# A fourth summed weight piece in every other gate-and-up unit, and summed pieces in half of u and in z

## The chip, the cores and the metric

The kernel runs on one core of one Trainium2 chip. The time is that of the device in microseconds (us). Engines are named as in the profile: PE is TensorE (matmuls; PEld its weight loads), DVE is VectorE, ACT is ScalarE, POOL is GpSimd, SP is SyncE, which here only issues DMAs.

## The reference

One layer of a hybrid decoder trunk, on 256 tokens of width 2048, all in float32:

```
h = x + 1/2 * SwiGLU_1(RMSNorm(x))                      # d_ff 5632: [2048 -> 2 x 5632], [5632 -> 2048]
P = RMSNorm(h) @ W_in                                   # columns: u 2048 | v 2048 | z 2048 | x 2048 | B 1024 | C 1024 | dt 32
a = gelu(u) * (W_s RMSNorm(gelu(v)) + b)                # causal mixing inside chunks of 128 tokens
m = RMSNorm(SSD(conv(x, B, C), dt) * SiLU(z))           # Mamba-2 chunked scan, 2 chunks of 128 tokens, 32 heads of 64
h = h + concat([a, m]) @ W_out
h = h + CrossAttn(RMSNorm(h), RMSNorm(mem))             # 4 heads of 512 into 256 memory tokens
h = h + 1/2 * SwiGLU_2(RMSNorm(h))
out = RMSNorm(h)
```

Weight gains of the norms and the conv's weights are left out here. The time goes into the big matrix products.

## The kernel before

**Products in three matmuls.** A float32 number is held as a rounded high part (type fp32r) and a remainder, the low part. A product of two such matrices takes three matmuls: high x high, high x low, low x high. Weights come from memory as float32 into a buffer `raw`; ScalarE writes the high part (`high`, L159 to L162) and VectorE the low part (`low`, L171 to L174, through `split_op`, which keeps these operations in the order in which they are written). Tokens are the stationary operand and weights the moving one, 512 columns a matmul. TensorE gets its instructions in program order (`pe`, L69).

**Units and pieces.** `proj_sum` (L245) works through one *unit*: two column blocks of 512 weights (j = 0, 1; gate and up, in an FFN) times two blocks of 128 tokens (t = 0, 1), over a contraction of 2048 in eight *pieces* of 256 (k = 0, 1, of 128 each). A piece is of one of two kinds.

- *C, plain*: the eight products (t, j, k), each of three matmuls: 24. One high and one low operation on 128x2048 weights.
- *S, summed*: Strassen and Winograd's scheme for 2 x 2 blocks, seven products, m1 to m7, for eight: 21 matmuls. For it VectorE makes four sums of the four weight blocks (tile `sum`, three operations), and highs and lows are made of three raw blocks and of the four sums (`split_sums`, L189). The token operand has the same sums, made beforehand (`Pieces.sums`, L415); its first four forms are the plain blocks, so that `tokens` (L239) can also read an S operand as a plain one.

Products m1, m6, m5, m7 each gather in a PSUM bank over all S pieces of the unit and are combined after the last of them (`mid`, four VectorE additions in `parts_of`); m2, m3, m4 gather in the banks of the plain results. In an S piece the products come in the order m1, m2, m3, m6, m5, m7, m4, in the last S of a unit m1, m6, m5, m7, m2, m3, m4 (L268 to L270). m1, m2 and m3 read raw weight blocks, the other four read sums. The unit ends with a C, in which each of the four results is evacuated (`evac`).

**Buffers.** Each pool has a fixed number of buffers, and a tile that is asked for waits until all that read the buffer's last content are done:

```
    wraw = ctx.enter_context(tc.tile_pool(name="wraw", bufs=3))
    whigh = ctx.enter_context(tc.tile_pool(name="whigh", bufs=3))
    wlow = ctx.enter_context(tc.tile_pool(name="wlow", bufs=2))
    wsum = ctx.enter_context(tc.tile_pool(name="wsum", bufs=1))
    wshigh = ctx.enter_context(tc.tile_pool(name="wshigh", bufs=1))
    wslow = ctx.enter_context(tc.tile_pool(name="wslow", bufs=1))
    big = ctx.enter_context(tc.tile_pool(name="big", bufs=12))
```

wsum, wshigh and wslow hold the sums of an S piece, their high and their low parts. `big` holds token operands and activations in twelve slots of 8 KB a partition; an S operand takes a slot, a C operand half of one.

**Order of work.** The kinds of a unit's pieces stand in a string, one letter for each piece of the contraction, and an order list says in which order the pieces are taken. GU_KINDS with GU_ORDER gives C C S C S C S C for all units of the FFNs but the first. An FFN has eleven units (c = 0 to 10); after five and after the other six, a down projection (`add_sum`, two halves) takes up their ten and twelve pieces. Small jobs (transposes that make the next operands, the steps of the scan) are put off with `later(fn, by)` by so many pieces, and `step` carries them out between pieces, but not between the first and the last S of a unit, when all PSUM banks are taken.

**The middle.** After FFN 1 come B, C and x (`proj_feat`), then v, u and z (`proj_tok`, all plain, eight pieces a half of 1024 columns, two halves each). The scan of the SSD runs beside v and u: `scan_start` (t, j) fetches a tile `dec` by a DMA of 1 MB and makes decays and scores, `scan_apply` does the matmuls yp and, at the end, yo. Then the output projection, the queries, the memory's keys and values, the attention and its output, and FFN 2.

Of the kernel before, what the change touches and what calls it, by code (L numbers as in the profile page):

```python
# [46 lines left out]
def hybrid_layer(ctx: ExitStack, tc: tile.TileContext, x, mem, w_gu1, w_dn1, w_in, w_s, w_out,  # L47
# [24 lines left out]
    def matmul(out, lhsT, rhs, start=False, stop=False):  # L72
        return pe(nc.tensor.matmul(out, lhsT=lhsT, rhs=rhs, start=start, stop=stop))  # L73
# [130 lines left out]
    def proj_tok(w, r0, xts, cs, evac, kts=D // P):  # L204

        n = kts // KP
        ps = {}
        for i in range(n):
            hi, lo = split(load(w, r0 + i * KP * P, cs, PLAIN))
            order = [(t, k) for k in range(KP) for t in range(NT)]  # L210
            if i in (0, n - 1):
                order.sort()
            for t, k in order:
                if t not in ps:
                    ps[t] = [side("acc") for _ in range(2)]
                kt = i * KP + k
                xt = xts[kt // KG][:, kt % KG, :]
                xh, xl = xt[:, t * P:(t + 1) * P], xt[:, S + t * P:S + (t + 1) * P]
# [106 lines left out]
        junk = half_k(F32, "junk")  # L325
        return nc.scalar.activation(junk, src, AF.Square, accum_out=ss)

    def rstd_of(ss, name):
        n = ss.shape[1]
        r = small.tile([P, n], F32, name=f"rstd_{name}", bufs=1)  # L330
        ms = small.tile([P, n], F32, name="ms")
        nc.vector.tensor_reduce(out=ms, in_=ss, axis=AX.X, op=ALU.add)
# [105 lines left out]
    class Normed:  # L438


        def __init__(self, name, c0, kinds=None, bys=None):
            self.bys = bys
            self.name, self.c0 = name, c0
            self.xts = [] if kinds is None else Pieces(kinds, f"xp_{name}")
            self.ss = small.tile([P, NT, 4], F32, name=f"ss_{name}", bufs=1)

        def chunk(self, n, by=1):
            srcs = [h[n][:, t, :] for t in range(NT)]
# [10 lines left out]
        def stats(self, n):  # L459
            for t in range(NT):  # L460
                sum_sq(self.ss[:, t, n:n + 1], h[n][:, t, :])
            if n == 3:
                self.rstd = rstd_of(self.ss, self.name)

    def axpy(y, a, x):
        return nc.vector.scalar_tensor_tensor(out=y, in0=x, scalar=a, in1=y, op0=ALU.mult, op1=ALU.add)
# [38 lines left out]
        nc.vector.tensor_tensor(out=out, in0=a, in1=b, op=op)  # L505
# [129 lines left out]
    def raw_dts():  # L635
# [5 lines left out]
        nc.vector.tensor_tensor(out=wd[:, :, HEADS:], in0=raw_dt, in1=wd[:, :, :HEADS].bitcast(F32), op=ALU.subtract)  # L641
        pdt = side("dt")
        for k in range(D // P):
            matmul(pdt[:2 * HEADS, :], wd[:, k, :], nx.xts[k // KG][:, k % KG, :],
                   start=(k == 0), stop=(k == D // P - 1))
        dtf = half_k(F32, "dtf")
        nc.scalar.copy(out=dtf[:2 * HEADS, :], in_=pdt[:2 * HEADS, :])
# [101 lines left out]
    dend = small.tile([P, HEADS], F32, name="dend", bufs=1)  # L749
    scan = {}  # L750

    def scan_start(t, j):
        hs = slice(j * 16, j * 16 + 16)
        if j == 0:
            scan["xdt"] = scan[f"xdt{t}"] = xdt = slot([P, HEADS, HD], F32, "xdt")
            nc.vector.tensor_tensor(out=xdt, in0=y[t], in1=per_head(dt[:, t, :], HD), op=ALU.mult)
            nc.vector.tensor_tensor(out=y[t], in0=y[t], in1=per_head(rowb[:, 2, :], HD), op=ALU.mult)
        dec = slot([P, 16, P], F32, "dec")
        nc.gpsimd.dma_start(
            out=dec.rearrange("p h l -> p (h l)"),  # L760
            in_=cum_rows[t:t + 1, j * 16 * P:(j + 1) * 16 * P].broadcast_to([P, 16 * P]))
# [101 lines left out]
    for c in (0, 2):  # L863
        gss = [[], []]

        def evac(t, ps):
            for j in range(2):
                g = half_k(F32, "gate")
                nc.scalar.activation(g, ps[j], AF.Gelu_apprx_tanh, scale=rstd[:, t:t + 1])
                nc.vector.scalar_tensor_tensor(out=g, in0=v[t][:, c + j, :],  # L870
                                               scalar=col[:, C_GB + c + j:C_GB + c + j + 1],
                                               in1=g, op0=ALU.add, op1=ALU.mult)
                gss[j].append(g)

        proj_tok(w_in, 0, nx.xts, (U0 + c * NC, U0 + (c + 1) * NC), evac)
        for j in range(2):
            ats.later(gss[j], by=1 + j)

    ss_m = small.tile([P, NT, 4], F32, name="ss_m", bufs=1)
    for c in (0, 2):  # L880
        def evac(t, ps):
            for j in range(2):
                g = half_k(F32, "gate")
                nc.scalar.activation(g, ps[j], AF.Silu, scale=rstd[:, t:t + 1])
                ys = y[t][:, (c + j) * 8:(c + j + 1) * 8, :].rearrange("p h d -> p (h d)")
                nc.vector.tensor_tensor(out=ys, in0=ys, in1=g, op=ALU.mult)
                sum_sq(ss_m[:, t, c + j:c + j + 1], ys)
# [44 lines left out]
    def heads(w, xps, kinds, order, c, take):  # L932
        parts = {}

        def mid(banks):
            parts.update(enumerate(parts_of(banks)))

        def evac(t, j, ps):
            x = parts[2 * t + j]
            total(x, ps, x, ALU.subtract if (t, j) == (1, 0) else ALU.add)  # L940
            take(j, t, x)

        proj_sum(w, 0, xps, kinds, (c, c + XD), mid, evac, order)

    MEM_KINDS = "CCCCCCSS"
    XA_ORDER, MEM_ORDER = [0, 1, 2, 5, 3, 7, 4, 6], [0, 1, 2, 6, 3, 7, 4, 5]
    qts, kts, mem_ts = [], [], Pieces(MEM_KINDS, "memt")

    def by_head(to, name):
# [7 lines left out]
        return take  # L957

    for hd in (0, 2):
        heads(w_q, na.xts, XA_KINDS, XA_ORDER, hd * XD, by_head(qts, "qt"))  # L960
# [36 lines left out]
        split_to(pts[hd // 2][:, hd % 2], tps)  # L997

    for hd in (0, 2):
        heads(w_kv, mem_ts, MEM_KINDS, MEM_ORDER, hd * XD, by_head(kts, "kt"))  # L1000
        for j in range(2):
            later(lambda hd=hd + j: attend(hd, kts[hd]), by=2 + j / 2)

# [19 lines left out]
    for hd in (0, 2):  # L1023
# [7 lines left out]
        heads(w_kv, mem_ts, MEM_KINDS, MEM_ORDER, D + hd * XD, take)  # L1031
# [91 lines left out]
```

## Time and profile before

| | |
|---|---|
| median of 2 runs | 2475.26 us (2474.72 to 2475.8) |
| the profiled execution | 2476.08 us, of it the span 2474.4 us |
| PE busy | 2457.2 us, 99% of the span, 11945 matmuls |
| DVE busy | 2027.1 us, 82% |
| ACT busy | 1303.0 us, 53% |
| weights and all else from memory | 472.57 MB read, 192 GB/s |

How to read the profile: times are from the start of the span. A group of instructions is given as line, engine, operation, output <- inputs, shape and count | busy us, mean ns of one | idle time of the engine ahead of them and what ended it. A time line gives start, duration, engine, line, operation and count, with the idle time ahead of it in brackets. The chain that ended last is followed back from the last instruction to what released each step. In a table of windows the row holds the window, its length, then PE, PEld, DVE, ACT and POOL busy (with counts), the granted clock, the DMA share and GB/s. L73 is the line of all matmuls, L161 of `high`, L169 of `split_op`.

### The profile page before, as it was taken

The numbers are of one execution on the slowest core, as the hardware profiler recorded it, in microseconds if no ns is written. First come the engines' busy times: TensorE is split into PE (matmuls) and PEld (weight loads), VectorE is DVE, ScalarE is ACT, GpSimd is POOL, SyncE is SP. The second block draws the span as 40 slices with busy tenths as digits, with TensorE's granted clock in tenths as the row PEclk, the third lists the DMA queues.
The fourth block names the chain that finished last, engine by engine and source line by source line (L and its number), as shares of the span: only waits on it lengthen the run. The fifth ranks groups of instructions, "written<-read, shape, count | busy, mean of one in ns | idle before, by whom it ended". The sixth has DMA issues, their size and how long they took to land.

```text
span 2474.4 us, 30190 instructions
## 1 busy us (share of the span) xinstructions
PE 2457.2 (99%) x11945; PEld 2069.2 (84%) x11945; DVE 2027.1 (82%) x1904; ACT 1303.0 (53%) x1180; POOL 21.0 (1%) x46
## 2 busy tenths in 40 slices
PE   9999999999999999999999999999999999999998
PEld 7888888888899998888888888888888888888886
DVE  7999889999877677655698888778789988899987
ACT  6555445555545454445555655455555544555554
POOL 0000000000000000000000000000000000000000
PEclk9999999999999999999999999999999999999999
DMA  7565665665654555545566555555565656656664
GB/s 241 190 211 191 206 201 192 204 201 190 201 184 162 192 177 202 204 153 187 187 199 227 191 183 170 169 172 185 179 197 193 213 192 202 204 188 204 204 206 151
DMA packets 199870, 476.67 MB, mean 193 GB/s; under 512 B 15296, under 2 KB 17504, under 8 KB 198960
## 3 DMA queue, kind: packets, MB, share of 16 engines
q1 hardware_dynamic: 196912, 464.31, 57.4%
q0 software_dynamic: 1840, 9.26, 1.1%
q8 instruction: 93, 1.52, 0.3%
q10 hardware_dynamic: 976, 1.18, 0.1%
q14 instruction: 49, 0.40, 0.0%
HBM read 472.57 MB, written 2.13 MB: 192 GB/s over the span
## 4 chain that ended last, share of the span: by engine, by line
PE 96%; DVE 2%; ACT 1%; issue 1%; DMA 0%; POOL 0%; DVEq 0%; ACTq 0%; POOLq 0%
PE acc L73 91%; PE tpose L76 2%; DVE lo L169 1%; PE yp L73 1%; ACT hi L161 1%; PE logits L73 0%; PE o L73 0%; DVE cacc L627 0%; PE mixed L73 0%; DMA col<-in_cols 0%; DVE sum L169 0%; PE dt L73 0%; PE scores L73 0%; PE yo L73 0%; PE st L73 0%
## 5 line engine op out<-in xcount | busy, mean ns | idle before, releaser
L161 ACT CAST hi<-raw 128x2048 fp32r<-128x2048 f32 (+1 forms) x438 | 788.2, 1800 | 819.3 <-PE acc L73 724.2
L169 DVE TENSOR_TENSOR lo<-raw,hi 128x2048 fp32r<-128x2048 f32 (+2 forms) x446 | 944.7, 2119 | 238.8 <-PE acc L73 183.8
L73 PE MATMUL acc<-hi,xp_ffn 128*128 128x512 f32 x1824 | 582.3, 392 | 1.5 <-ACT hi L183 1.5
L73 PEld LDWEIGHTS acc<-hi,xp_ffn 128*128 128x128 f32 x1824 | 343.6, 188 | 72.9 <-ACT hi L183 2.2
L73 PE MATMUL acc<-lo,xp_ffn 128*128 128x512 f32 x912 | 356.1, 390 | 0.2 <-DVE lo L169 0.2
L169 DVE TENSOR_TENSOR lo<-sum,hi 128x2048 fp32r<-128x2048 f32 x117 | 268.2, 2292 | 59.4 <-ACT hi L161 59.4
L161 ACT CAST hi<-sum 128x2048 fp32r<-128x2048 f32 x117 | 224.1, 1915 | 119.8 <-DVE sum L169 100.5
L73 PE MATMUL acc<-hi,hid 128*128 128x512 f32 x896 | 282.6, 390 | 0.0
L73 PE MATMUL acc<-hi,xt_mix 128*128 128x512 f32 x768 | 241.7, 393 | 0.0
L73 PEld LDWEIGHTS acc<-lo,xp_ffn 128*128 128x128 f32 x912 | 171.9, 188 | 35.5 <-DVE lo L169 0.7
L505 DVE TENSOR_TENSOR part<-acc,part 128x512 f32<-128x512 f32 x272 | 180.4, 686 | 24.5 <-ACT part L472 9.3
L73 PEld LDWEIGHTS acc<-hi,hid 128*128 128x128 f32 x896 | 168.3, 188 | 34.7
L73 PE MATMUL acc<-xt_mix,hi 128*128 128x256 f32 x1024 | 185.9, 284 | 0.0
L73 PE MATMUL acc<-lo,hid 128*128 128x512 f32 x448 | 174.6, 390 | 0.0
L73 PEld LDWEIGHTS acc<-hi,xt_mix 128*128 128x128 f32 x768 | 144.2, 188 | 30.3 <-issue 0.7
L169 DVE TENSOR_TENSOR sum<-sum,raw 128x512 f32<-128x512 f32 x234 | 161.6, 690 | 6.6
L73 PEld LDWEIGHTS acc<-xt_mix,hi 128*128 128x128 f32 x1024 | 159.6, 192 | 0.3
L73 PE MATMUL acc<-lo,xt_mix 128*128 128x512 f32 x384 | 149.6, 389 | 0.0
L73 PE MATMUL acc<-hi,xp_ffn1s 128*128 128x512 f32 x466 | 148.5, 389 | 0.0
L73 PE MATMUL acc<-hi,xp_ffn2s 128*128 128x512 f32 x466 | 148.5, 389 | 0.0
L73 PE MATMUL acc<-xt_mix,lo 128*128 128x256 f32 x512 | 145.2, 284 | 0.7 <-DVE lo L169 0.7
L169 DVE TENSOR_TENSOR sum<-raw 128x1024 f32<-128x1024 f32 x117 | 142.5, 1218 | 0.0
(280 smaller groups left out, 3205.0 us busy)
## 6 DMA issues: line engine op xcount, KB each, us to landing
raw<-in_w_gu SPq DMA_DIRECT2D x286, 512.0 KB, 4.0
raw<-in_w_in SPq DMA_DIRECT2D x80, 1024.0 KB, 5.2
raw<-in_w_dn SPq DMA_DIRECT2D x60, 1024.0 KB, 5.2
raw<-in_w_gu SPq DMA_DIRECT2D x132, 256.0 KB, 4.1
raw<-in_w_kv SPq DMA_DIRECT2D x24, 1024.0 KB, 5.2
raw<-in_w_out SPq DMA_DIRECT2D x21, 1024.0 KB, 5.2
raw<-in_w_dn SPq DMA_DIRECT2D x28, 512.0 KB, 3.9
raw<-in_w_dn SPq DMA_DIRECT2D x56, 256.0 KB, 4.3
```

The costliest lines, as they stand in the source:

```text
L73: return pe(nc.tensor.matmul(out, lhsT=lhsT, rhs=rhs, start=start, stop=stop))
L76: return pe(nc.tensor.transpose(out=out, in_=in_, identity=identity))
L161: nc.scalar.copy(out=t[:, :n], in_=x[:, :n])
L169: last_split[:] = [nc.vector.tensor_tensor(**kw).ins]
L505: nc.vector.tensor_tensor(out=out, in0=a, in1=b, op=op)
```

## The change

- Units c = 2, 4, 6, 8, 10 of both FFNs: four S pieces for three, in the order C C S S C S S C. Units c = 1, 3, 5, 7, 9 stay at C C S C S C S C; unit 0 stays as it is but reads operand 6, which is now of kind S, as a plain one.
- Down projections of five blocks: two S pieces for three. The FFN's operand (four S, four C) and these ten pieces (two S, eight C) take six slots each.
- The second half of u and both halves of z: `proj_sum` with two S pieces (C C C S C S C C) in place of `proj_tok`, through `column_pair`, which is the `heads` of the attention moved ahead. The operand of the middle becomes a list of Pieces with two S, five slots in place of four; its sums of squares are taken three steps after FFN 1 has ended.
- The scan's starts and applications go from steps 3, 7, 13, 17 and 7, 10, 17, 21 to 5, 8, 15, 18 and 8, 11, 18, 21. Its first two VectorE operations become `scan_inputs`, a step ahead, and `dec` goes from the pool `big` to `wshigh`.
- Queries, keys and values: other orders of the same pieces.

```diff
-    GU_KINDS, GU_ORDER = "CSCSCSCC", [0, 2, 1, 4, 3, 6, 5, 7]
+    GU_KINDS, GU_ORDER = "CSCSCSSC", [0, 2, 1, 4, 3, 6, 5, 7]
+    GU_THREE, MORE_ORDER = "CSCSCSCC", [0, 2, 1, 3, 4, 5, 6, 7]
...
-    DN_KINDS = {5: ("CCSCSCSCCC", None), 6: ("CCCCSCCSCCSS", [0, 1, 4, 2, 10, 3, 7, 5, 11, 6, 8, 9])}
+    DN_KINDS = {5: ("CCSCCSCCCC", None), 6: ("CCCCSCCSCCSS", [0, 1, 4, 2, 10, 3, 7, 5, 11, 6, 8, 9])}
...
                 if c == 0:
                     proj_sum(w_gu, 0, nrm.xts, FIRST_KINDS, (c * NC, DFF + c * NC), mid, evac, FIRST, fine)
+                elif c % 2:
+                    proj_sum(w_gu, 0, nrm.xts, GU_THREE, (c * NC, DFF + c * NC), mid, evac, GU_ORDER)
                 else:
-                    proj_sum(w_gu, 0, nrm.xts, GU_KINDS, (c * NC, DFF + c * NC), mid, evac, GU_ORDER)
+                    proj_sum(w_gu, 0, nrm.xts, GU_KINDS, (c * NC, DFF + c * NC), mid, evac, MORE_ORDER)
...
-    nx = Normed("mix", C_MIX)
+    MIX_KINDS = "CCCSCSCC"
+    nx = Normed("mix", C_MIX, MIX_KINDS, {4: 1, 5: 1, 6: 2, 7: 2})
...
+    def scan_inputs(t):
+        scan["xdt"] = scan[f"xdt{t}"] = xdt = slot([P, HEADS, HD], F32, "xdt")
+        nc.vector.tensor_tensor(out=xdt, in0=y[t], in1=per_head(dt[:, t, :], HD), op=ALU.mult)
+        nc.vector.tensor_tensor(out=y[t], in0=y[t], in1=per_head(rowb[:, 2, :], HD), op=ALU.mult)
...
-        dec = slot([P, 16, P], F32, "dec")
+        dec = wshigh.tile([P, 16, P], F32, name="hi")
...
-    for i, (by, to) in enumerate(((3, 7), (7, 10), (13, 17), (17, 21))):
+    for i, (by, to) in enumerate(((5, 8), (8, 11), (15, 18), (18, 21))):
+        if i % 2 == 0:
+            later(lambda i=i: scan_inputs(i // 2), by=by - 1)
...
-        proj_tok(w_in, 0, nx.xts, (U0 + c * NC, U0 + (c + 1) * NC), evac)
+        if c == 0:
+            proj_tok(w_in, 0, nx.xts, (U0 + c * NC, U0 + (c + 1) * NC), evac)
+        else:
+            column_pair(w_in, nx.xts, MIX_KINDS, None, U0 + c * NC, lambda j, t, x: gate(j, t, x, x))
...
-        proj_tok(w_in, 0, nx.xts, (Z0 + c * NC, Z0 + (c + 1) * NC), evac)
+        column_pair(w_in, nx.xts, MIX_KINDS, None, Z0 + c * NC, take)
...
-    XA_ORDER, MEM_ORDER = [0, 1, 2, 5, 3, 7, 4, 6], [0, 1, 2, 6, 3, 7, 4, 5]
+    XA_ORDER, MEM_ORDER = [0, 1, 2, 3, 5, 4, 7, 6], [0, 1, 2, 3, 6, 4, 7, 5]
```

With the query kinds CCCCCSCS and the memory kinds CCCCCCSS the last line turns C C C S C S C C into C C C C S C S C.

More of the change, by code (lines that the diff above doesn't have):

```diff
@@ L326, in sum_sq, with rstd_of @@
         return nc.scalar.activation(junk, src, AF.Square, accum_out=ss)
-    def rstd_of(ss, name):
+    def rstd_of(ss, name, r=None):
         n = ss.shape[1]
-        r = small.tile([P, n], F32, name=f"rstd_{name}", bufs=1)
+        r = small.tile([P, n], F32, name=f"rstd_{name}", bufs=1) if r is None else r
         ms = small.tile([P, n], F32, name="ms")
@@ L445, in __init__ @@
             self.ss = small.tile([P, NT, 4], F32, name=f"ss_{name}", bufs=1)
+            self.rstd = small.tile([P, NT], F32, name=f"rstd_{name}", bufs=1)
         def chunk(self, n, by=1):
@@ L462, in stats @@
             if n == 3:
-                self.rstd = rstd_of(self.ss, self.name)
+                rstd_of(self.ss, self.name, self.rstd)
     def axpy(y, a, x):
@@ L505, in total, with column_pair, mid, evac @@
         nc.vector.tensor_tensor(out=out, in0=a, in1=b, op=op)
-    GU_KINDS, GU_ORDER = "CSCSCSCC", [0, 2, 1, 4, 3, 6, 5, 7]
+    def column_pair(w, xps, kinds, order, c, take):
+        parts = {}
+        def mid(banks):
+            parts.update(enumerate(parts_of(banks)))
+        def evac(t, j, ps):
+            x = parts[2 * t + j]
+            total(x, ps, x, ALU.subtract if (t, j) == (1, 0) else ALU.add)
+            take(j, t, x)
+        proj_sum(w, 0, xps, kinds, (c, c + NC), mid, evac, order)
+    GU_KINDS, GU_ORDER = "CSCSCSSC", [0, 2, 1, 4, 3, 6, 5, 7]
+    GU_THREE, MORE_ORDER = "CSCSCSCC", [0, 2, 1, 3, 4, 5, 6, 7]
     FIRST_KINDS, FIRST = "CCCCCSCC", [0, 2, 4, 6, 1, 3, 5, 7]
-    DN_KINDS = {5: ("CCSCSCSCCC", None), 6: ("CCCCSCCSCCSS", [0, 1, 4, 2, 10, 3, 7, 5, 11, 6, 8, 9])}
+    DN_KINDS = {5: ("CCSCCSCCCC", None), 6: ("CCCCSCCSCCSS", [0, 1, 4, 2, 10, 3, 7, 5, 11, 6, 8, 9])}
     def ffn(nrm, w_gu, w_dn, done=None, each=None, fine=0):
@@ L643, in raw_dts @@
         for k in range(D // P):
-            matmul(pdt[:2 * HEADS, :], wd[:, k, :], nx.xts[k // KG][:, k % KG, :],
+            x, i = nx.xts[k // KP], k % KP
+            x = x[:, :, 2 * i:2 * i + 2].rearrange("p h f s -> p h (f s)") if len(x.shape) == 4 else \
+                x[:, i].rearrange("p (h s) -> p h s", h=2)
+            matmul(pdt[:2 * HEADS, :].rearrange("p (h s) -> p h s", h=2), wd[:, k, :], x,
                    start=(k == 0), stop=(k == D // P - 1))
@@ L864, in hybrid_layer, with gate @@
         gss = [[], []]
+        def gate(j, t, g, x):
+            nc.scalar.activation(g, x, AF.Gelu_apprx_tanh, scale=rstd[:, t:t + 1])
+            nc.vector.scalar_tensor_tensor(out=g, in0=v[t][:, c + j, :],
+                                           scalar=col[:, C_GB + c + j:C_GB + c + j + 1],
+                                           in1=g, op0=ALU.add, op1=ALU.mult)
+            gss[j].append(g)
         def evac(t, ps):
             for j in range(2):
[L868 to L873, printed above, removed]
-        proj_tok(w_in, 0, nx.xts, (U0 + c * NC, U0 + (c + 1) * NC), evac)
+                gate(j, t, half_k(F32, "gate"), ps[j])
+        if c == 0:
+            proj_tok(w_in, 0, nx.xts, (U0 + c * NC, U0 + (c + 1) * NC), evac)
+        else:
+            column_pair(w_in, nx.xts, MIX_KINDS, None, U0 + c * NC, lambda j, t, x: gate(j, t, x, x))
         for j in range(2):
@@ L880, in hybrid_layer, with take @@
     for c in (0, 2):
[L881 to L887, printed above, removed]
-        proj_tok(w_in, 0, nx.xts, (Z0 + c * NC, Z0 + (c + 1) * NC), evac)
+        def take(j, t, g):
+            nc.scalar.activation(g, g, AF.Silu, scale=rstd[:, t:t + 1])
+            ys = y[t][:, (c + j) * 8:(c + j + 1) * 8, :].rearrange("p h d -> p (h d)")
+            nc.vector.tensor_tensor(out=ys, in0=ys, in1=g, op=ALU.mult)
+            sum_sq(ss_m[:, t, c + j:c + j + 1], ys)
+        column_pair(w_in, nx.xts, MIX_KINDS, None, Z0 + c * NC, take)
     rstd_m = rstd_of(ss_m, "m")
@@ L929, in prep_mem @@
         return ms
[L932 to L943, printed above, removed]
     MEM_KINDS = "CCCCCCSS"
-    XA_ORDER, MEM_ORDER = [0, 1, 2, 5, 3, 7, 4, 6], [0, 1, 2, 6, 3, 7, 4, 5]
+    XA_ORDER, MEM_ORDER = [0, 1, 2, 3, 5, 4, 7, 6], [0, 1, 2, 3, 6, 4, 7, 5]
     qts, kts, mem_ts = [], [], Pieces(MEM_KINDS, "memt")
@@ L959, in hybrid_layer @@
     for hd in (0, 2):
-        heads(w_q, na.xts, XA_KINDS, XA_ORDER, hd * XD, by_head(qts, "qt"))
+        column_pair(w_q, na.xts, XA_KINDS, XA_ORDER, hd * XD, by_head(qts, "qt"))
         if hd == 0:
@@ L999, in hybrid_layer @@
     for hd in (0, 2):
[L1000 removed]
+        column_pair(w_kv, mem_ts, MEM_KINDS, MEM_ORDER, hd * XD, by_head(kts, "kt"))
         for j in range(2):
@@ L1029, in take @@
                                     op=ALU.subtract)
-        heads(w_kv, mem_ts, MEM_KINDS, MEM_ORDER, D + hd * XD, take)
+        column_pair(w_kv, mem_ts, MEM_KINDS, MEM_ORDER, D + hd * XD, take)
         for j in range(2):
```

7 lines of the change are left out of this document (1 added, 6 removed).

## The prediction

> **What bounds the kernel now.** I read the page first: busy times, then the chain that ended last.
>
> ```profile
> PE 2457.2 (99%) x11945; PEld 2069.2 (84%) x11945; DVE 2027.1 (82%) x1904; ACT 1303.0 (53%) x1180; POOL 21.0 (1%) x46
> PE 96%; DVE 2%; ACT 1%; issue 1%; DMA 0%; POOL 0%; DVEq 0%; ACTq 0%; POOLq 0%
> ```
>
> TensorE is the chain (96%) and leaves 2474.4 - 2457.2 = 17.2 us of the span unused. So a matmul that goes saves its time, and a wait that reaches TensorE costs its whole length; nothing later absorbs it. Next the chain in order of time, in the first half-step FFN, then the windows of two gate-and-up units:
>
> ```profile
> 65.41 41.50 PE acc L73 x183
> 107.79 41.50 PE acc L73 x183
> 150.16 41.50 PE acc L73 x183
> ...
> 65.40:107.80 42.40, 42.40 (x193) 35.20 (x192) 38.26 (x33) 22.45 (x17) 0.00 (x0) 1.00 0.60 198
> 107.80:150.20 42.40, 42.40 (x192) 35.19 (x192) 39.61 (x37) 23.59 (x19) 0.00 (x0) 1.00 0.61 199
> ```
>
> A unit takes 42.37 us, of which 183 matmuls take 41.50, or 0.2268 us each; the rest is eight transposes. 183 = 3 x 21 + 5 x 24: three summed pieces (S, seven products of three matmuls) and five plain ones (C, eight of three). So C costs 5.44 us of TensorE, S 4.76, and one piece turned from C to S saves 0.68. VectorE (third figure) is busy 38.3 to 39.6 of 42.4 us: it keeps up with little to spare. What it and ScalarE do for one piece:
>
> ```profile
> L161 ACT CAST hi<-sum 128x2048 fp32r<-128x2048 f32 x117 | 224.1, 1915 | 119.8 <-DVE sum L169 100.5 <-PE acc L73 19.0
> L169 DVE TENSOR_TENSOR lo<-sum,hi 128x2048 fp32r<-128x2048 f32 x117 | 268.2, 2292 | 59.4 <-ACT hi L161 59.4
> L169 DVE TENSOR_TENSOR lo<-raw,hi 128x2048 fp32r<-128x2048 f32 x321 | 734.7, 2289 | 234.0 <-PE acc L73 178.9 <-issue 45.7 <-ACT hi L161 3.8
> L169 DVE TENSOR_TENSOR lo<-raw,hi 128x1536 fp32r<-128x1536 f32 x117 | 205.0, 1752 | 4.8 <-PE acc L73 4.8
> L169 DVE TENSOR_TENSOR sum<-raw 128x1024 f32<-128x1024 f32 x117 | 142.5, 1218 | 0.0
> L169 DVE TENSOR_TENSOR sum<-sum,raw 128x512 f32<-128x512 f32 x234 | 161.6, 690 | 6.6
> ```
>
> S costs VectorE 1.22 + 2 x 0.69 + 1.75 + 2.29 = 6.64 us, C 2.29. The 19.0 us of ScalarE waiting for PE in the first row is the clue to this change: the rounded sums (hi<-sum, from the pool wshigh) and their remainders (lo<-sum, from wslow) have one buffer each, so those of the next S cannot be written before TensorE is done with the last. The time line of the down projection shows such a wait:
>
> ```profile
> 307.29 0.39 PE L73 MATMUL acc<-hi,hids 128*128 128x512 f32 x1
> 307.52 0.39 PE L73 MATMUL acc<-hi,hid 128*128 128x512 f32 x1
> 307.76 1.92 ACT L161 CAST hi<-sum 128x2048 fp32r<-128x2048 f32 x1 [0.85 <-PE acc L73]
> 309.71 2.29 DVE L169 TENSOR_TENSOR lo<-sum,hi 128x2048 fp32r<-128x2048 f32 x1 [0.43 <-ACT hi L161]
> ...
> 1247.69 2.30 DVE lo L169
> 1250.04 54.49 PE acc L73 x239
> ```
>
> The last matmul of an S (tile hids) starts at 307.29 and ends at 307.68; the next piece, a C, starts at T = 307.52. The cast starts at T + 0.24 and ends at T + 2.16, the remainders run from T + 2.19 to T + 4.48, and a matmul follows such a remainder after some 0.04 us (the last two rows, from the chain): T + 4.52. Here the C's 5.44 us of matmuls cover it. In the kernel before, every S is followed by a C.
>
> **The change, part by part.**
>
> *Two S in a row.* The units c = 2, 4, 6, 8, 10 of both FFNs get the kinds C C S S C S S C in the order of MORE_ORDER. The pools and split_sums stay, so in each pair the second S pays the chain above with only its own matmuls as cover, on a TensorE queue in program order. Its sums are first read as the remainder operand of product m6. Product order m1, m2, m3, m6 puts that matmul behind ten others, at T + 10 x 0.2268 = T + 2.27: a stall of 4.52 - 2.27 = **2.25 us**. The last S of a unit has the order m1, m6: behind four, T + 0.91, a stall of **3.61 us**. Nothing else in the pair comes later: counted from the start of the unit's second C, the first S ends at 10.2; the rows below, 3.4 and 4.4 us after the starts of two chain pieces above, have VectorE done with its remainders at 6.7 at the latest, and so with the second's three sums and raw remainders (4.35 us, and 0.7 for a block's operand) by 11.8, ahead of the cast's end at 12.4. At the last pair the same count leaves the sums ready 1 us before the cast may start.
>
> ```profile
> 112.23 2.29 DVE L169 TENSOR_TENSOR lo<-sum,hi 128x2048 fp32r<-128x2048 f32 x1 [0.66 <-ACT hi L161]
> 153.60 2.29 DVE L169 TENSOR_TENSOR lo<-sum,hi 128x2048 fp32r<-128x2048 f32 x1 [0.73 <-ACT hi L161]
> ```
>
>  Behind the waiting cast on ScalarE stands the next C's cast (1.91 us), and on VectorE that C's remainder: ready 2.2 us after the sums' remainder, while the second S has 2.5 or 3.9 us of matmuls left. So the wait isn't passed on. A unit: -0.68 + 2.25 + 3.61 = +5.18 us; ten units: **+51.8 us**. The lower bound is no reuse wait: -6.8.
>
> *Fewer and more S elsewhere.* Down projections of five blocks drop from three S to two, in two halves of two FFNs: 4 x 0.68 = **+2.7**. One half of u and both of z get two S each, with a C between: 6 x 0.68 = **-4.1**. There VectorE gains per half two S for C (8.7 us) and eight 128x512 additions of 0.69, 42.6 us in all; the window of the three halves has 132.0 - 69.3 = 62.7 us of its time free. Without that cover TensorE would wait for the excess. The summed weights come as three transfers, not one of 1 MB, on SP's queue; the DMA share of 0.58 hides it.
>
> ```profile
> 1090.00:1222.00 132.00, 132.00 (x592) 109.27 (x590) 69.28 (x54) 64.18 (x63) 0.71 (x1) 1.00 0.58 187
> ```
>
> *Orders of the query and memory projections* (S one place later) can at best remove these two waits:
>
> ```profile
> 1414.55 0.50 PE L73 MATMUL acc<-lo,xp_xas 128*128 128x512 f32 x1 [1.20 <-DVE lo L169]
> 1498.29 0.73 PE L73 MATMUL acc<-hi,memts 128*128 128x512 f32 x2 [1.10 <-DVE memts L430]
> ```
>
> At best -2.3, at worst a new wait of the same size; I take **-2.0**, since both operands are made just ahead of use.
>
> *The scan.* dec moves from the big pool to wshigh, one buffer, so the transfer for a token block's second half waits for the first half's yp matmuls. The fourth dec did that already:
>
> ```profile
> 1020.39 3.52 PE yp L73 x32
> 1023.91 0.95 PE scores L73 x8
> 1030.31 1.72 PE mixed L73 x4
> ...
> 1024.20 0.53 POOL L759 DMA_DIRECT2D dec<-cum_rows  x1 [3.09 <-PE yp L73]
> 1031.19 2.29 DVE L764 TENSOR_TENSOR dec<-dec,cum 128x2048 f32<-128x2048 f32 x1 [6.55 <-DMA dec<-cum_rows]
> 1036.80 4.48 DVE L169 TENSOR_TENSOR lo<-raw,hi 128x2048 fp32r<-128x2048 f32 x2
> ```
>
> VectorE's subtraction starts 10.8 us after yp, and the next piece's remainder stands behind it; "mixed" matmuls filled TensorE. The second dec, now at step 8, has no such filler: after yp, scores and two pieces TensorE reaches the third at 3.52 + 0.95 + 2 x 5.44 = 15.4, and VectorE ends subtraction, minimum and remainder at 10.8 + 3 x 2.25 = 17.5. About **+2** (0 if the remainder is put first, 4 if the other halves meet it too). On POOL's queue the third dec (step 15) still goes before the gate's wn loads, which are asked for after step 16, and the fourth (18) behind them; SP's queue has none of these.
>
> *Statistics after FFN 1.* As a list of Pieces, the mix operand takes its sums of squares at step 3, the step of spread_rstd; before they were taken at once, 14 us ahead of the matmul rb:
>
> ```profile
> 720.22 0.16 DVE L332 TENSOR_REDUCE ms<-ss_mix 128x2 f32<-128x8 f32 x1 [1.68 <-ACT junk L326]
> 734.79 0.45 PE rb L73 x4
> ```
>
> ScalarE and VectorE run about two pieces ahead of TensorE, which hides most of it; **+1** (0 to 4). z's heavier end, with the output projection's operands right behind it, **+1** (0 to 3); the S form of operand 6 in the crowded first unit **+0.5** (0 to 1.5).
>
> **Sum:** 51.8 + 2.7 - 4.1 - 2.0 + 2 + 1 + 1 + 0.5 = +52.9. The profiled execution took 2476.1 us (span 2474.4 and 1.7 around it), 0.8 over the median of the runs: 2529.0 profiled, and **2528** as the median.
>
> **The rivals.** *The reuse wait doesn't bind* (not slower). If the second S's sums could be cast while the first is still multiplied, only the matmuls would count: twelve more S, -8.2, and the small terms +2.5: **2470**. From 2.27 us of the 4.52 being free it decides: then each pair costs nothing. For it: VectorE's 42.6 to 44.0 us of work in a four-S unit still nearly fits. Against it: the cast at 307.76 started 0.08 us after the end of the last hids matmul, 0.85 us after ScalarE was free. Chance 0.13.
>
> *VectorE's order at the unit's end.* If the four additions on m1, m6, m5, m7 are queued before the last C's remainder, that one waits for m7 (2.0 us after the sums' remainder), a 0.58 us copy and one or two additions, and ends some 1.4 us after TensorE wants it. Ten units: +14, **2542**. In the trace the remainders go first:
>
> ```profile
> 133.45 2.29 DVE L169 TENSOR_TENSOR lo<-raw,hi 128x2048 fp32r<-128x2048 f32 x1
> 136.11 1.49 DVE L505 TENSOR_TENSOR part<-acc,part 128x512 f32<-128x512 f32 x2 [0.36 <-ACT part L472]
> ```
>
> Chance 0.08.
>
> *The clock falls in the gaps.* At the program's start matmuls run at half pace:
>
> ```profile
> 10.97 1.05 PE L73 MATMUL acc<-hi,xp_ffn 128*128 128x512 f32 x2
> 11.82 0.63 PE L73 MATMUL acc<-lo,xp_ffn 128*128 128x512 f32 x1
> ```
>
> Two in 0.85 us, 0.43 each, and so from 9.4 to 15.2 us: 2.9 us lost. One such stretch in each of ten units is +29: **2557**. The two gaps of a unit are at most 2.3 us, and the longer stall is cut in two by m6's first matmul (1.3 and 2.1 us). Chance 0.06. [...]
>
> **How the numbers follow.** Forecast 0.70, its own range 2521 to 2543 (the small terms at their ends, and 2 us on the pairs); rivals 0.13, 0.08, 0.06; 0.03 for the rest. 2514 to 2557 holds 0.69 + 0.08 + 0.03 = 0.80; its low end lets each of the twenty pairs be 0.35 us cheaper than I count. Two per cent, about what a measurement of this kernel can tell from no change, is 49.5 us: 2524.8 lies just under the forecast, three quarters of whose range is above it. Slower: 0.75 x 0.70 + 0.08 + 0.06 = 0.66; same: 0.18 + 0.13 + 0.01 = 0.32; faster by 2%: nothing here gives it, 0.02.
>
> **What would show it.** In the changed profile, even units of 47.5 us and odd ones of 42.4; PE waits for lo (L169) of about 1.9 to 2.1 us, one in each of twenty pairs, and for hi (L161) of 1.3 us in the last pair of a unit; about 36 matmuls fewer; casts hi<-sum that wait for PE far longer than 19.0 us. Even units of 41.7 would prove the first rival, lo waits at the unit's last C the second, matmuls at 0.43 us after a gap the third. The forecast is wrong if the scheduler or the pools give the sums a second home that I don't see, and its side of 2% turns on 3 us of small terms.

## The result, and the profile after

The changed kernel takes **2561.3 us** (2557.59 to 2565.01), against 2475.26: a ratio of 1.0346 (interval 1.0329 to 1.0363), 3.5% slower. The forecast was 2528 us, the range 2514 to 2557. The profiled execution took 2557.59 us, of it a span of 2555.9, 81.5 us longer than before; the sum of the prediction was 52.9.

The page of the kernel after, with the rows that answer to those shown of before: busy times, chain, and the two groups of the sums.

```profile
PE 2484.4 (97%) x11909; PEld 2075.1 (81%) x11909; DVE 2093.7 (82%) x1979; ACT 1323.3 (52%) x1200; POOL 23.3 (1%) x46
PE 88%; DVE 6%; ACT 3%; issue 2%; DMA 1%; POOL 0%; ACTq 0%; POOLq 0%; DVEq 0%; SPq 0%
L161 ACT CAST hi<-sum 128x2048 fp32r<-128x2048 f32 x129 | 246.7, 1913 | 138.7 <-DVE sum L169 108.3
L169 DVE TENSOR_TENSOR lo<-sum,hi 128x2048 fp32r<-128x2048 f32 x129 | 295.6, 2291 | 96.4 <-ACT hi L161 96.2
```

There are the 36 fewer matmuls that were counted, and TensorE is nevertheless busy 27.2 us longer: at 0.2268 us each the 36 should have saved 8.2. That is the first sign that many matmuls ran slower. What TensorE leaves of the span grew from 17.2 to 71.5 us, and the chain of VectorE and ScalarE from 3% to 9% of the span. The waits of TensorE (us in total, times, longest) name the operations: the first row is of before, the other two of after.

```profile
PE acc L73 <- DVE lo L169: 2.6, 6, 1.2
PE acc L73 <- DVE lo L169: 44.5, 38, 3.0
PE acc L73 <- ACT hi L161: 13.2, 10, 1.6
```

There are forty-eight waits after, ten of them for a high part: those are the last pairs of the ten four-S units. Next the windows of the kernel after. The first two rows are a four-S unit and the three-S unit behind it; the other five lie in the four-S unit c = 4 and are stretches of 3.41 us.

```profile
107.10:156.88 49.78, 44.45 (x191) 35.27 (x189) 43.78 (x40) 24.91 (x20) 0.00 (x0) 0.97 0.50 164
156.88:199.25 42.37, 42.37 (x194) 35.17 (x193) 39.85 (x38) 23.57 (x19) 0.00 (x0) 1.00 0.62 206
211.02:214.43 3.41, 1.59 (x7) 0.83 (x6) 2.69 (x2) 0.69 (x1) 0.00 (x0) 1.00 0.84 297
214.43:217.85 3.42, 3.42 (x10) 2.68 (x9) 3.39 (x3) 1.48 (x1) 0.00 (x0) 0.50 0.14 14
228.09:231.50 3.41, 1.77 (x7) 0.91 (x5) 0.81 (x1) 2.38 (x2) 0.00 (x0) 1.00 0.83 247
231.50:234.91 3.41, 1.87 (x8) 1.58 (x9) 3.41 (x2) 0.00 (x0) 0.00 (x0) 1.00 0.15 60
234.91:238.33 3.42, 3.42 (x17) 2.83 (x16) 3.31 (x4) 1.79 (x1) 0.00 (x0) 1.00 0.53 140
```

The four-S unit takes 49.78 us where 47.55 was forecast, and its granted clock (the third figure from the end) is 0.97. In the fourth row the clock is 0.50, and TensorE, busy all the time, gets through ten matmuls where the last row has 17. Before, that column was 1.00 in every unit.

The first wait of the unit c = 4 is the one that the prediction worked out. Its cast of the sums, remainder, and TensorE's product m6, in the time line of after:

```profile
209.80 1.91 ACT L161 CAST hi<-sum 128x2048 fp32r<-128x2048 f32 x1 [1.28 <-PE acc L73]
211.74 2.29 DVE L169 TENSOR_TENSOR lo<-sum,hi 128x2048 fp32r<-128x2048 f32 x1 [2.07 <-ACT hi L161]
214.08 0.52 PE L73 MATMUL acc<-lo,xp_ffn1s 128*128 128x512 f32 x1 [1.82 <-DVE lo L169]
```

The cast waits for TensorE, and the matmul that needs the remainder starts 4.28 us after the cast: exactly the T + 0.24 to T + 4.52 of the working. So it is in the first pair of all ten four-S units: m6's second matmul starts there at T + 4.52 or T + 4.53. The last pair of the unit c = 2 differs:

```profile
132.29 1.42 DVE L169 TENSOR_TENSOR sum<-sum,raw 128x512 f32<-128x512 f32 x2
133.81 1.91 ACT L161 CAST hi<-raw 128x2048 fp32r<-128x2048 f32 x1 [1.71 <-DVE sum L169]
134.51 0.61 PE L73 MATMUL acc<-hi,xp_ffn1s 128*128 128x512 f32 x2
135.44 0.50 PE L73 MATMUL acc<-lo,xp_ffn1s 128*128 128x512 f32 x1 [0.31 <-DVE lo L169]
135.62 1.89 ACT L161 CAST hi<-sum 128x2048 fp32r<-128x2048 f32 x1
137.54 2.29 DVE L169 TENSOR_TENSOR lo<-sum,hi 128x2048 fp32r<-128x2048 f32 x1 [2.16 <-ACT hi L161]
137.56 0.50 PE L73 MATMUL acc<-hi,xp_ffn1s 128*128 128x512 f32 x1 [1.40 <-ACT hi L161]
139.89 0.79 PE L73 MATMUL acc<-lo,xp_ffn1s 128*128 128x512 f32 x1 [1.83 <-DVE lo L169]
140.48 1.05 PE L73 MATMUL acc<-hi,xp_ffn1s 128*128 128x512 f32 x2
```

The second S starts with the second matmul of the third row, at T = 134.74. Its sums are ready at 133.71, yet ScalarE takes the cast of the *next C* at 133.81, and the sums' cast follows it at 135.62, 0.64 us later than T + 0.24, with no idle time of its own. m6's second matmul starts at T + 5.15 instead of T + 4.52. In all ten last pairs the next C's cast goes ahead in this way, but it does not always cost something: in units 4 and 6 of both FFNs it has ended before the buffer comes free, and m6 starts at T + 4.52; in units 2 and 8 of both and in unit 10 of the first it runs over, and m6 starts between T + 4.87 and T + 5.15. In unit 10 of the second FFN m6 starts at T + 4.80, with the C's cast out of the way; the reason isn't seen. And behind the wait two matmuls take 0.86 us (140.48 to 141.34): half pace, in the stretch of half clock that begins at 139.34.

### The profile page after: what moved, and what is told of

Its sections match the earlier page's. It is cut to its first block, busy times and chain, and to the rows that moved or that the text cites. A ratio compares the mean times of both kernels' runs of the same rounds, so it can differ in the third digit from the quotient of the medians.

```text
span 2555.9 us, 30231 instructions
## 1 busy us (share of the span) xinstructions
PE 2484.4 (97%) x11909; PEld 2075.1 (81%) x11909; DVE 2093.7 (82%) x1979; ACT 1323.3 (52%) x1200; POOL 23.3 (1%) x46
## 4 chain that ended last, share of the span: by engine, by line
PE 88%; DVE 6%; ACT 3%; issue 2%; DMA 1%; POOL 0%; ACTq 0%; POOLq 0%; DVEq 0%; SPq 0%
PE acc L73 83%; DVE lo L169 3%; ACT hi L161 2%; PE tpose L76 2%; DVE sum L169 1%; DMA raw<-in_w_gu 1%; DMA hi<-cum_rows 1%; PE o L73 0%; PE logits L73 0%; DVE cacc L645 0%; PE yp L73 0%; PE mixed L73 0%; ACT junk L325 0%; PE dt L73 0%; DVE hi L794 0%
## 5 line engine op out<-in xcount | busy, mean ns | idle before, releaser
L73 PE MATMUL acc<-hi,xp_ffn 128*128 128x512 f32 x1408 | 448.8, 392 | 0.0
L161 ACT CAST hi<-sum 128x2048 fp32r<-128x2048 f32 x129 | 246.7, 1913 | 138.7 <-DVE sum L169 108.3
L73 PEld LDWEIGHTS acc<-hi,xp_ffn 128*128 128x128 f32 x1408 | 265.0, 188 | 55.2 <-ACT hi L183 0.4
L73 PE MATMUL acc<-lo,xp_ffn 128*128 128x512 f32 x704 | 274.7, 390 | 0.2 <-DVE lo L169 0.2
L73 PEld LDWEIGHTS acc<-hi,hid 128*128 128x128 f32 x1024 | 192.2, 188 | 39.7
L73 PE MATMUL acc<-hi,xp_ffn1s 128*128 128x512 f32 x632 | 208.3, 405 | 6.4 <-ACT hi L161 6.4
L505 DVE TENSOR_TENSOR part<-acc,part 128x512 f32<-128x512 f32 x296 | 195.5, 685 | 22.0 <-PE acc L73 7.8
L73 PE MATMUL acc<-hi,xp_mix 128*128 128x512 f32 x576 | 182.0, 391 | 0.0
L73 PEld LDWEIGHTS acc<-hi,xp_ffn2s 128*128 128x128 f32 x632 | 124.0, 196 | 35.9 <-ACT hi L161 10.0
L73 PEld LDWEIGHTS acc<-hi,xp_ffn1s 128*128 128x128 f32 x632 | 123.4, 195 | 35.1 <-ACT hi L161 9.6
L73 PE MATMUL acc<-lo,xp_ffn1s 128*128 128x512 f32 x316 | 129.2, 409 | 21.0 <-DVE lo L169 20.9
L73 PE MATMUL acc<-lo,xp_ffn2s 128*128 128x512 f32 x316 | 129.7, 410 | 18.8 <-DVE lo L169 18.8
L73 PE MATMUL acc<-xp_mix,hi 128*128 128x256 f32 x768 | 140.1, 284 | 0.0
```

The lines of the kernel that those rows point to most:

```text
L161: nc.scalar.copy(out=t[:, :n], in_=x[:, :n])
```

## The experiments

Two theories stood at first. *Buffer and clock*: the reuse wait of the single wshigh and wslow buffers costs what was worked out, and the rest is half-clock stretches behind the gaps. *Something else in the four-S units or the middle* carries the excess. All times below are medians beside runs of the kernel before on the same chip (2475.58 and 2475.59 us).

### Three S in all units, the rest of the change kept

```diff
-                    proj_sum(w_gu, 0, nrm.xts, GU_KINDS, (c * NC, DFF + c * NC), mid, evac, MORE_ORDER)
+                    proj_sum(w_gu, 0, nrm.xts, GU_THREE, (c * NC, DFF + c * NC), mid, evac, GU_ORDER)
```

> The changed kernel with three summed pieces, C C S C S C S C, in every gate-and-up unit; the operand's layout, the down projections, the middle and the scan stay as changed. Theory (two S in a row cost the buffer wait, and the clock falls in the gaps): all units back at 42.37 us, no half-clock stretch in the FFNs; 2475.3 + 2.7 for the down projections and about 0 for the middle = 2478 us, between 2473 and 2482. Rival (the layout, the middle or the scan carry part of the loss): 2490 us or more.

2480.02 us (2477.34 to 2483.47), ratio 1.0018 (1.0008 to 1.0027). The four-S units carry 81.3 of the 85.7 us by which the changed kernel is slower than before on this count; the rest of the change costs 4.4, where 1.1 was forecast. The largest wait in it is one at the scan, in the time line of this kernel:

```profile
936.17 0.18 DVE L785 TENSOR_TENSOR dend<-hi,cum 128x16 f32<-128x16 f32 x1 [3.29 <-DMA hi<-cum_rows]
936.39 2.29 DVE L786 TENSOR_TENSOR hi<-hi,cum 128x2048 f32<-128x2048 f32 x1
938.60 2.28 DVE L775 TENSOR_TENSOR xdt<-y,dt 128x2048 f32<-128x2048 f32 x1
940.80 2.28 DVE L787 TENSOR_TENSOR hi<-hi,sum 128x2048 f32<-128x2048 f32 x1
943.00 2.28 DVE L776 TENSOR_TENSOR y<-y,rowb 128x2048 f32<-128x2048 f32 x1
945.21 2.28 DVE L169 TENSOR_TENSOR lo<-raw,hi 128x2048 fp32r<-128x2048 f32 x1
947.54 0.52 PE L73 MATMUL acc<-lo,xp_mixs 128*128 128x512 f32 x1 [4.10 <-DVE lo L169]
```

VectorE waits 3.3 us for the *first* dec, then does four scan operations of 2.28 us ahead of a remainder that TensorE wants: TensorE waits 4.1 us.

### Zero matmuls in the pairs' waits

Only TensorE's idle time is to be taken away: a block of zeros is multiplied into the same bank where m6 waits, six and eight times in a unit's last pair, eight times in the first.

```diff
+                for _ in range(fill[1].get(m, 0) if fill else 0):
+                    matmul(banks[name], zeros, fill[0])
...
+                    if name == "m6" and kinds[order[m - 1]] == "S":
+                        fill = (parts[0][0], {0: 6, 1: 8} if m == s_at[-1] else {1: 8})
```

> The changed kernel with matmuls by a tile of zeros, which add nothing, put where TensorE waits in a pair of S: eight ahead of m6's second matmul, and in the last pair of a unit six more ahead of its first. The buffer wait itself stays. Theory (the clock falls because of the idle gaps): no half-clock stretch is left in the FFNs, a four-S unit takes 47.4 to 48.2 us (the filler is 0.8 us too long in units 2 and 8), total 2561.3 - 27 + 3 = about 2537 us. Rival (the rest over my forecast is VectorE's order or load, the clock costs nothing): 2561 us or more.

2542.9 us (2540.05 to 2544.6), ratio 1.0275 (1.0258 to 1.0292): 18.4 us less than the changed kernel, with 220 more matmuls. The window of its unit c = 2, the one that took 49.78 us:

```profile
106.69:155.24 48.55, 47.58 (x214) 38.52 (x212) 43.71 (x40) 24.98 (x20) 0.00 (x0) 1.00 0.52 168
```

The clock is 1.00 and the unit 1.2 us shorter, though the operand of m6 comes no sooner: 32.86 us after the unit's start here (the row below, from the time line), 32.79 in the changed kernel.

```profile
139.55 0.50 PE L73 MATMUL acc<-lo,xp_ffn1s 128*128 128x512 f32 x1
```

So the clock's share is shown, some 18 us at least. The four-S units still cost 2542.9 - 2480.02 = 62.9 us, 6.3 each, 1.1 more than the 5.18 forecast. Not all of this is the wait's: in the first pairs of units 2 and 8 the zero matmuls last longer than the wait and hold m6 back until T + 5.35, and the cast order, which differs here, lets m6 of the last pairs start anywhere from T + 4.53 (unit 2, the row above) to T + 5.78.

### A second home for the second S's sums, in units 2, 6 and 8

```diff
-        t = pool.tile([P, 2 * KP, NC], F32R, name="hi")
+        t = slot([P, 2 * KP, NC], F32R, "hi2") if pool is None else pool.tile([P, 2 * KP, NC], F32R, name="hi")
...
-        thi = high(wshigh, t, 4)
-        tlo = low(wslow, t, thi, 4)
+        thi = high(None if apart else wshigh, t, 4)
+        tlo = low(None if apart else wslow, t, thi, 4)
```

> The changed kernel in which the second S of a pair writes its rounded sums and their remainders to two free slots of the big pool, in units 2, 6 and 8 of both FFNs; units 4 and 10 stay as they are, for comparison. Theory (reuse of the single buffers is the wait): the six units fall from 49.4 to 52.0 to between 41.7 us (matmuls alone) and 44 us (VectorE's work), the other four stay at 49 to 52; total about 2515 to 2527 us. Rival (VectorE's load of four S holds the unit, whatever the buffers): the six units stay above 46 us, total over 2540 us.

2556.8 us (2555.83 to 2562.1), ratio 1.0333 (1.0318 to 1.0348). That is 30 us and more above what was expected. With the buffer free the first pair's wait shrank (in unit 6 from 2.1 to 0.8 us, by the matmuls' starts), but the last pair's stayed. Its time line in unit 2:

```profile
131.21 1.42 DVE L169 TENSOR_TENSOR sum<-sum,raw 128x512 f32<-128x512 f32 x2
132.76 1.91 ACT L161 CAST hi<-raw 128x2048 fp32r<-128x2048 f32 x1 [1.68 <-DMA raw<-in_w_gu]
134.58 1.89 ACT L161 CAST hi<-sum 128x2048 fp32r<-128x2048 f32 x1
136.50 2.29 DVE L169 TENSOR_TENSOR lo<-sum,hi 128x2048 fp32r<-128x2048 f32 x1 [2.20 <-ACT hi L161]
138.85 0.50 PE L73 MATMUL acc<-lo,xp_ffn1s 128*128 128x512 f32 x1 [1.83 <-DVE lo L169]
```

The sums are ready at 132.63, and no buffer holds their cast. The next C's cast goes ahead of it again and costs it 1.95 us. So "the single buffer" was not the whole cause: behind it ScalarE's order binds at almost the same moment. That made a new theory, with two edits to test it.

### The same, and the next C's cast put behind the sums'

```diff
-                with behind(xps.made[i] if m < fine else ()):
+                after_pair = [kinds[i] for i in order[max(m - 2, 0):m]] == ["S", "S"]
+                with behind(xps.made[i] if m < fine else list(cast) if after_pair else ()):
```

(`cast` holds the last cast that `high` wrote.)

> e5_home with one order more: ScalarE casts the C that follows a pair of S only after the second S's sums. New theory: in the last pair of e5_home the sums were ready at 132.6 us but their cast began at 134.58, behind the next C's cast, which had waited for its weights; besides the buffer, the chain sums, cast, remainder (2.6 + 1.9 + 2.3 us) on VectorE and ScalarE holds the second S. Expected: the last pair's wait in units 2, 6 and 8 falls by about 2 us (from 3.6 to 1.6) and their clock mostly stays up: those six units 45 to 47.5 us, total 2535 to 2545 us. Rival (the order on ScalarE is not the bound): six units stay at 49 to 50, total 2550 to 2562 us.

2532.77 us (2527.11 to 2536.86), ratio 1.0223 (1.0207 to 1.0239): 24 us less than with the second home alone. By the matmuls' starts in the two profiles, about half of that is shorter waits in units 2, 6 and 8 and half is clock (a mean of 0.990, with the second home alone 0.983). The same place in unit 2:

```profile
131.53 1.42 DVE L171 TENSOR_TENSOR sum<-sum,raw 128x512 f32<-128x512 f32 x2
132.98 1.91 ACT L163 CAST hi<-sum 128x2048 fp32r<-128x2048 f32 x1 [5.07 <-DVE sum L171]
134.92 2.29 DVE L171 TENSOR_TENSOR lo<-sum,hi 128x2048 fp32r<-128x2048 f32 x1 [0.31 <-ACT hi L163]
137.27 0.50 PE L73 MATMUL acc<-lo,xp_ffn1s 128*128 128x512 f32 x1 [1.64 <-DVE lo L171]
```

The cast follows the sums at once, and one wait is left of two. Units 2, 6 and 8 take 44.8 to 46.1 us, one of them 47.6. Units 4 and 10, which have the cast order but not the second home, take 49.4 to 52.2 us, as in the changed kernel. So ScalarE's order was the second bound, and in these pairs neither of the two edits does it alone. The remaining 1.64 us is the third: sums, cast and remainder take 2.7 + 1.9 + 2.3 us one behind the other, and in the last order m6 asks for their result after four matmuls.

### More cover for m6: the usual product order in the last S of a pair

The changed kernel, with one line:

```diff
-                if m == s_at[-1]:
+                if m == s_at[-1] and kinds[order[m - 1]] != "S":
                     names = ["m1", "m6", "m5", "m7", "m2", "m3", "m4"]
```

> The changed kernel with the products of a unit's last S in the order m1, m2, m3, m6, m5, m7, m4 where an S stands before it: ten matmuls ahead of the first use of the sums' remainder, not four. Theory (matmuls of the second S are the cover of the wait): the last pair's wait falls by 6 x 0.2268 = 1.36 us to some 2.3 us, in one gap of about 2.1 us that drops the clock in four of ten units, not nine; total 2561.3 - 13.6 - 10 = about 2538 us. Rival (the wait is not measured from the second S's start): 2552 us or more.

2531.77 us (2530.82 to 2533.5), ratio 1.0225 (1.0209 to 1.0241): 29.5 us less than the changed kernel, more than expected. Six more matmuls ahead of m6 are 1.36 us a unit, 13.6 in all. Most of the rest goes with the clock (a mean of 0.995, in the changed kernel 0.988), as two units of this kernel (c = 2 and c = 8) with the same work show:

```profile
106.29:155.06 48.77, 44.77 (x192) 35.44 (x190) 42.28 (x38) 24.84 (x20) 0.00 (x0) 0.97 0.48 156
483.82:530.55 46.73, 42.91 (x192) 34.31 (x190) 42.00 (x38) 24.85 (x20) 0.00 (x0) 1.00 0.50 163
```

Their waits differ by 0.2 us in sum, and one unit is 2.04 us longer: it has a half-clock stretch in it, at 140.06, and the other has none.

### Only one pair, at the unit's start (C S S C S C S C)

```diff
-    GU_THREE, MORE_ORDER = "CSCSCSCC", [0, 2, 1, 3, 4, 5, 6, 7]
+    GU_THREE, MORE_ORDER = "CSCSCSCC", [0, 1, 3, 2, 5, 4, 6, 7]
```

> The changed kernel with the order C S S C S C S C in the four-S units: one pair of S, not the last. Theory: a unit costs -0.68 + 2.25 = +1.6 us of wait, with one gap of 2.1 us, which drops the clock in about four of ten units (2 us each); 2475.3 + 2.7 + 15.7 + 8 = 2502 us, 2494 if a gap of 2.1 us never drops it. Rival (the fourth S as such is too much for VectorE): 2520 us or more.

2515.9 us (2514.0 to 2518.51), ratio 1.0164 (1.0149 to 1.0179). Better than two pairs by 45 us, yet 14 over what was expected: units of 45.1 to 47.3 us. Right behind the unit's first C the pair meets VectorE still making operands for the down projection (hids, hid), and then short of time for three remainders in a row:

```profile
115.09 1.75 DVE L169 TENSOR_TENSOR lo<-raw,hi 128x1536 fp32r<-128x1536 f32 x1
116.76 2.29 DVE L169 TENSOR_TENSOR lo<-sum,hi 128x2048 fp32r<-128x2048 f32 x1
116.89 0.50 PE L73 MATMUL acc<-lo,xp_ffn1s 128*128 128x512 f32 x1 [2.39 <-DVE lo L169]
```

Here TensorE waits for the raw remainder, not for that of the sums: the first bound of this pair is VectorE's time. The buffer is not out of it: in three of the ten units m6 starts at the T + 4.52 that the buffer sets, in the others up to T + 5.31.

### Second home, cast order and product order together

```diff
+        thi = high(None if apart else wshigh, t, 4)
...
+                with behind(xps.made[i] if m < fine else list(cast) if after_pair else ()):
...
+                if m == s_at[-1] and kinds[order[m - 1]] != "S":
```

> e7_order with the product order of e8_names: the second home in units 2, 6, 8, the sums' cast first, and ten matmuls of cover. Theory: what is left in units 2, 6 and 8 is VectorE's work for four S, 42.6 to 44.0 us; these units take 42.5 to 45 us with no half-clock stretch, so not below the 42.37 us of three S; units 4 and 10 about 47.5 us; total 2505 to 2520 us. Rival (buffer, order and cover were all): six units at 41.7 us, total under 2500 us.

2511.48 us (2509.59 to 2514.84), ratio 1.0146 (1.0132 to 1.016). Its units c = 6 and c = 2:

```profile
388.95:432.46 43.51, 42.75 (x192) 34.31 (x190) 40.57 (x34) 23.52 (x18) 0.00 (x0) 1.00 0.54 175
106.91:151.59 44.68, 42.95 (x191) 34.30 (x189) 42.00 (x38) 24.53 (x20) 0.00 (x0) 1.00 0.52 170
```

In units 2, 6 and 8 all three edits act and the clock stays up, and a four-S unit still takes 43.5 to 44.7 us, above the 42.37 of three S. (Units 4 and 10, without the second home, take 46.5 to 48.1.) What TensorE still waits for in unit 6 is VectorE, three times 0.25 us, each time for a remainder. A fourth S saves TensorE 0.68 us and costs VectorE 6.64 - 2.29 = 4.35, and the three-S unit has 2.8 to 4.1 of VectorE's time to spare. That this forbids the gain is argued, not shown: VectorE is busy only 40.6 to 42.0 us in these units, and unit 6 hands work on to the next, where it is busy 39.7 of 42.37 us.

### The middle alone, with dec's operations a step behind its transfer

The FFNs and down projections of before. The transfer of dec keeps its step, VectorE's operations on it come a step later, and they stand behind the newest remainder.

```diff
+        with behind(last_split):
...
+            nc.vector.tensor_tensor(out=dec, in0=dec, in1=per_head(cum[:, t, hs], P), op=ALU.subtract)
...
-        later(lambda i=i: scan_start(i // 2, i % 2), by=by)
+        later(lambda i=i: scan_fetch(i // 2, i % 2), by=by)
+        later(lambda i=i: scan_start(i // 2, i % 2), by=by + 1)
```

> The FFNs of the kernel before (three S, the operand and down projections as before) with the changed middle, and the scan's transfer asked for a step ahead of its VectorE operations, which go behind the newest remainder. e1_three had 2480.0 us, of which 2.7 are the down projections; its one long wait (4.1 us at 947.5, VectorE's four scan operations ahead of a remainder, and the half-clock stretch after it) and 1.1 us at yp make some 7 us. Theory (summed pieces in u and z gain 4.1 us and the scan's order ate them): 2470 to 2474 us, below the kernel before. Rival (u and z gain nothing): 2476 us or more.

**2469.76 us** (2468.75 to 2473.45), ratio 0.9979 (0.997 to 0.9988): it is faster than both kernels, by 5.8 us or 0.2% against the kernel before. VectorE's order at the first dec, and TensorE's waits for remainders in the whole of this kernel:

```profile
935.67 2.29 DVE L169 TENSOR_TENSOR lo<-raw,hi 128x2048 fp32r<-128x2048 f32 x1
937.87 0.17 DVE L789 TENSOR_TENSOR dend<-hi,cum 128x16 f32<-128x16 f32 x1
938.08 2.29 DVE L790 TENSOR_TENSOR hi<-hi,cum 128x2048 f32<-128x2048 f32 x1
```

```profile
PE acc L73 <- DVE lo L169: 3.3, 8, 1.1
```

The wait for the DMA is gone, a remainder stands ahead of the operations on dec, and TensorE no longer waits for a remainder there (the wait of 1.1 lies in the first unit of FFN 1). Which of the two edits did it is not told apart. The 5.8 us fit what the matmuls and waits give: 18 matmuls fewer in u and z are 4.1 us, and the waits of 1.20 and 1.10 us at the query and memory projections, which the prediction showed, are gone too. So the summed pieces in u and z do pay; in the changed kernel the scan's order ate their gain.

## Why the prediction was right and wrong

Of the 85.7 us between the medians of the changed kernel and of the kernel before on that chip, 4.4 are for all but the four-S units and 81.3 for these; forecast were 1.1 and 51.8. What the 81.3 consist of can be counted in the profile of the changed kernel: a matmul that starts more than 0.2268 us after the one before it is late by the excess. In the ten units the matmuls at TensorE's waits are late by 59.3 us in sum, where ten times 2.25 + 3.61 = 58.6 was forecast. Matmuls in stretches of half clock are late by 22.6, forecast as nothing. The rest, 4.2, also forecast as nothing, is mostly the first matmul behind each wait, about 0.1 us late (214.08 to 214.42 is 0.34 us, not 0.23). Less the 6.8 of the saved matmuls, that is 79.3 us in the profiled execution.

- **The clock: the step that failed, and what put the time out of the range.** The sum held nothing for it, and the rival got 0.06: that gaps of at most 2.3 us are too short for it was the author's guess, which no run had shown. One gap was enough: the wait ahead of 214.08, 2.1 us by the matmuls' starts and 1.82 by the profile (211.02:214.43 above). The profile counts 22.6 us in half-clock stretches, and filling the gaps gave 18.4 us back, with costs of its own. The price for one stretch, 2.9 us taken from the start of the program, was too high: a stretch is 3.41 us at half pace, at most 1.7, and some units have two or three. The rival's sum of 2557 came near partly by luck: it had 29 us for the clock, too much, and lacked some 5 at and behind the waits and 3 in the rest of the change.
- **Two S in a row: right in kind and in size, wrong in one step.** T + 4.52 came out to the hundredth in all ten first pairs and in four last pairs, and the odd units stayed at 42.37. The wrong step is "Behind the waiting cast on ScalarE stands the next C's cast": it stands *ahead* of it in the last pairs. In unit 2 that made 3.61 us into 0.47 + 0.10 + 1.57 + 2.10 = 4.24 (the delays of m1's and m6's matmuls against a matmul every 0.2268 us); over the ten units it made some 2.4 us. The expectation of "casts that wait for PE far longer" missed: of the 138.7 us that these casts wait after, all but 108.3 is for PE, 30.4 against 19.0 before. And the buffer alone wasn't the cause: with a second home the last pair waited as before. Counted from the start of unit 2, the sums' cast could start at 27.88 us by the buffer (134.98 - 107.10), started at 27.98 with a second home (134.58 - 106.60) and at 26.06 with the cast order mended too (132.98 - 106.92): two bounds lie 0.1 us apart, and the third, the sums themselves, 1.9 us ahead of them.
- **The matmul counts held**: 36 fewer matmuls, and the six S more in u and z paid once the scan was out of their way. The query and memory orders removed their two waits, as forecast. The other small terms were not told apart. A down projection with the unit ahead of it takes 190.83 us in the three-S kernel and 189.47 before: twice 1.36 us is the forecast +2.7.
- **The scan was mis-sized and misplaced.** +2 was taken at the second dec, with VectorE's subtraction 10.8 us after yp. It was the first dec, whose transfer came late for VectorE, and TensorE waited 4.1 us in the three-S kernel and 2.95 in the changed one, with a stretch of half clock behind it (up to 1.7 more); the time line of after, and the window of that stretch below the one of unit c = 2:

```profile
983.22 2.28 DVE L169 TENSOR_TENSOR lo<-raw,hi 128x2048 fp32r<-128x2048 f32 x1
985.56 0.57 PE L73 MATMUL acc<-lo,xp_mixs 128*128 128x512 f32 x1 [2.95 <-DVE lo L169]
```

```profile
139.34:142.75 3.41, 2.86 (x7) 2.28 (x8) 3.31 (x4) 0.00 (x0) 0.00 (x0) 0.50 0.15 59
985.85:989.26 3.41, 3.41 (x9) 2.64 (x9) 3.41 (x2) 0.00 (x0) 0.00 (x0) 0.50 0.78 229
```

- **The other rivals.** That the reuse wait doesn't bind is out: the cast waited for TensorE, and m6 started 4.28 us after it. VectorE's order at the unit's end did not turn: the next C's remainder runs at 139.75, and the additions of `mid` (L505) follow at 141.96.

## What to carry to other kernels

Before one plain step is exchanged for one that spares the bound engine a little and costs the second one much, compare the second engine's free time with its price in the same unit: here 2.8 to 4.1 us against 4.35, and none of the buffers and orders tried won the exchange. When a wait on a buffer is found, ask what stands behind it (the next engine's order, then the chain's own length) before a second buffer is expected to pay. And price a gap on TensorE with the clock: here a wait of 2.1 us cost its own length and up to 1.7 us more.

## What was not expected of the hardware

The granted clock fell to half behind single gaps of TensorE as short as 2.1 us (211.02:214.43, 1.59 us of 3.41 busy), and not behind gaps of 1.5 and 2.1 us whose idle time a boundary at 231.50 cut in two, with 1.77 and 1.87 us busy on its two sides (228.09 to 234.91). In the profile of the changed kernel every stretch of half clock between the first 30 and the last 40 us lasts 3.41 us or twice that (2405.79:2412.62, at 0.50), and all start on one grid: those at 139.34, 214.43 and 985.85 lie 75.09 and 771.42 us apart, 22 and 226 times 3.413. If the profile is cut into windows on this grid, half clock follows on all 13 windows at full clock in which TensorE is busy for at most 1.59 us. Of the 4 at full clock that are busy for 1.63 to 1.77 us it follows on one (426.06:429.47, 1.71), and on none of those above that; 2 windows at half clock themselves, with 1.81 and 1.94 us busy, are followed by another. So the same wait costs up to 1.7 us more or nothing, by where it falls: of the six first pairs with an undivided wait of 2.1 us five are followed by half clock, and that of unit 10 of the first FFN (596.73:600.14, 1.63 us busy) is not. The two executions of the changed kernel, 2557.59 us at a mean clock of 0.988 and 2565.01 at 0.985, may differ by that. One stretch is not explained by a gap: in the fastest kernel the clock is at 0.50 in the window below, and from 976.30 to 986.50 TensorE is busy for 9.50 of 10.20 us, idle only for the 0.70 us that the scan's yp matmuls of 64 columns wait. Behind the same matmuls of the kernel before the clock stays at 1.00 (1020.00:1030.00 and 1053.00:1062.00); what sets it off stays open.

```profile
982.80:986.20 3.40, 3.40 (x11) 2.86 (x11) 2.39 (x2) 0.00 (x0) 0.53 (x1) 0.50 0.98 334
```
